# A differential-attention block: the gate multiplied on GpSimd as a group's values leave PSUM, and scores in chunks of 1024, 1024 and 256 keys

## The chip, the cores and the metric

The kernel runs on one core of a Trainium2 chip. The metric is the time on the device in microseconds, from the first to the last instruction and what lies around them. The core's engines work from queues of their own and meet at semaphores: TensorE (products and transposes into PSUM), VectorE, ScalarE and GpSimd (work on elements), and SyncE (SP), which here issues all DMA transfers.

## The reference

One block of a diffusion transformer with differential attention: 2048 latent tokens, 256 context tokens, a model width of 1024, 8 heads. Each head has two query and key maps of width 64 and values of width 128. Both softmaxes run over all 2304 keys.

```python
s = jnp.einsum('bqhzd,bkhzd->bhzqk', q, k)
p = jax.nn.softmax(s, axis=-1)
a = p[:, :, 0] - lam * p[:, :, 1]
o = jnp.einsum('bhqk,bkhe->bqhe', a, v)
...
of = of * lax.rsqrt(jnp.mean(of * of, axis=-1, keepdims=True) + SUBLN_EPS)
of = of * subln_gain * (1.0 - lambda_init)
y = (of.reshape(B, L, D) * jax.nn.silu(z)) @ w_out
...
return rms_norm(x + gt * y, final_gain)
```

Ahead of it stand a norm with modulation, one projection of width 4096 (queries, keys, values and the gate's z) and an axial rotation of queries and keys. All arithmetic has the accuracy of float32.

## The kernel before, in words

**Three stages.** `project` writes queries, keys, values and the gate (silu of z times `sgain`, transposed) to DRAM. `attend` computes the attention. `finish` multiplies by the output weights, adds x and applies the last norm.

**Attention.** A group is 256 queries of a head (`GQ`); there are 8 groups a head and 64 in all. A group consists of two halves `u` of 128 queries, and each half has two maps `z`; one half with one map is called a unit here. For a unit, `qk` (L671) computes the scores of 2304 keys in three chunks of 768. A chunk takes a score buffer of two PSUM banks; there are two such buffers (`S_BUFS`). Operands are split into a high and a low part, so each piece of keys gets two products (`f` = 0, 1), each of 384 columns. `keep` (L697) brings a chunk from PSUM to SBUF on VectorE and finds its least value on the way. `least`, `expo` (ScalarE, over all 2304 keys), `ratio`, then `weigh` and `join` on GpSimd (L726, L731) form the difference of both softmaxes.

The difference is then turned, 128 by 128, by TensorE (`turn`, L735; nine blocks a group), split into `hi` (ScalarE) and `lo` (VectorE, L751), and multiplied by the values in `pv` (L756) with products of 256 columns. After the ninth block `evac` (L768) copies the group's 128x256 result out of PSUM and stores it to `o_d`. `clamp`, `square`, `sq_high`, `sq_low` (GpSimd, L785), `sumsq` and `ssq_out` form the sum of squares, a row of which is stored for each group. At the end of a head `root` (GpSimd, nine small instructions from L823 to L831) turns the head's sums into factors, which `f_out` stores to `f_d`.

**Output.** For a block of 512 queries and each head, `Last.load` fetches the result, the gate and the factors into one of two sets of buffers (`o`, `gate`, `f`), 256 KB each. `mul1` (L968) multiplies by the factors on GpSimd, `mul2` (L972) by the gate on VectorE, `high` (L976) and `low` (L982) split the product into `gh` (ScalarE) and `gl` (VectorE). In `finish`, `mm` (L1020) multiplies with the output weights, with 512 columns. Heads 0 to 6 of the first block are prepared beside the attention of head 7; the others follow in `finish`.

**Order.** Each stage is written as steps with an engine, a cost in ns, a due time, dependencies and buffers to take and give. `Plan.order` (L128) plays these through and so fixes each engine's order once; `in_order` (L182) makes it binding. A letter in a plan stands for a pool of buffers: S the score buffers, T the blocks of `turn`, A and B the unit's scores, O the buffers of `Last`. Due times in `attend` count units of a third of a unit (`PER` = 12 a group). SP issues in the order in which the steps were written out, and waits at each transfer until its data and its buffer are ready.

Of the kernel before, what the change touches and what calls it, by code (L numbers as in the profile page):

```python
# [20 lines left out]
P = 128  # L21
# [4 lines left out]
KEYS = LAT + CTX  # L26
# [7 lines left out]
LN2 = math.log(2.0)  # L34
G = 2
GQ = G * P
CK = 768
NC = KEYS // CK
# [16 lines left out]
def build(tc, x, c, ctx, c_ctx, norm_gain, ada_w, ada_b, final_gain, w_in,  # L55
          lam_q, lam_k, subln_gain, w_out, cos_t, sin_t, out):
    nc = tc.nc
    with ExitStack() as top:
# [36 lines left out]
        last = Last(tc, gate_d, o_d, f_d, wo_d)  # L95
        ph = top.enter_context(ExitStack())
        with ExitStack() as inner:
            attend(tc, ph, inner, early, last, ident, ones, mhalf, sums, neglam, q_d, k_d, v_d, o_d, s_d, f_d)
# [94 lines left out]
def project(tc, ph, attend_early, ones, x, ctx, c, c_ctx, norm_gain, ada_w, ada_b, w_in, lam_q, lam_k, subln_gain,  # L193
# [296 lines left out]
    def z_gain(nm):  # L490
        nc.gpsimd.tensor_scalar(tiles["z", nm], tiles["z", nm], sgain[:, 0:1], 1.0, op0=ALU.mult, op1=ALU.mult)
# [151 lines left out]
def attend(tc, ph, inner, early, last, ident, ones, mhalf, sums, neglam, q_d, k_d, v_d, o_d, s_d, f_d):  # L643
# [27 lines left out]
    def qk(g, u, z, ck):  # L671
# [13 lines left out]
        for f in range(2):  # L685
            for b in range(2):
                k0 = ck * CK + b * (CK // 2)
                nc.tensor.matmul(ps[:, b, :CK // 2], group[g].q[:, z, f, u * P:(u + 1) * P],  # L688
                                 head[h].k[:, z, k0:k0 + CK // 2], start=(f == 0), stop=(f == 1))
                yield  # L690
# [6 lines left out]
    def keep(g, u, z, ck):  # L697
        un = unit[g, u]
        nc.vector.tensor_scalar(  # L699
            un.p[z][:, ck * CK:(ck + 1) * CK].rearrange("p (b k) -> p b k", b=2),  # L700
            un.s[z, ck][:, :, :CK // 2], -0.125, None, op0=ALU.mult, op1=ALU.min,
            accum_out=un.st[:, 3 * z + ck:3 * z + ck + 1])
# [32 lines left out]
    def turn(g, b):  # L735
        pt = ps_t.tile([P, 512], F32, tag="t", name=f"t{g}_{b}")
# [31 lines left out]
    def evac(g):  # L768
# [3 lines left out]
        nc.sync.dma_start(o_d[h][:, i * GQ:(i + 1) * GQ], group[g].o)  # L772

    def clamp(g):
        group[g].sq = op.tile([P, GQ], F32, tag="sq", name=f"sqo{g}")
        nc.gpsimd.tensor_scalar(group[g].sq, group[g].o, 2.0 ** 59, -(2.0 ** 59), op0=ALU.min, op1=ALU.max)

# [43 lines left out]
    def root(h):  # L821
# [4 lines left out]
        nc.gpsimd.tensor_scalar(hd.mk, hd.u, 2.0 ** 72, 1.0, op0=ALU.is_lt, op1=ALU.mult)  # L826
# [15 lines left out]
    plan = Plan(S=S_BUFS, T=T_BUFS, A=A_BUFS, B=2, HI=TP_BUFS, LO=TP_BUFS, O=2)  # L842
# [15 lines left out]
    for g in range(TOTAL):  # L858
        h = g // NG
        for u in range(G):  # L860
            for z in range(2):
                s0 = g * PER + (u * 2 + z) * NC
                for ck in range(NC):
                    take = ["S"] + (["AB"[z]] if ck == 0 else [])
                    step("qk", "PE", 700, s0 + ck, qk, (g, u, z, ck), take=take)
                    step("keep", "DVE", 865, s0 + ck + 0.5, keep, (g, u, z, ck), [("qk", g, u, z, ck)],
# [18 lines left out]
        step("clamp", "Pool", 1029, due + 6, clamp, (g,), [("evac", g)])  # L885
        step("square", "Activation", 307, due + 7, square, (g,), [("clamp", g)])
# [14 lines left out]
    for h in range(H - 1):  # L901
# [4 lines left out]
        step("gmul2", "DVE", 602, due + 5, last.mul2, (0, h), [("gmul1", 0, h)])  # L906
        step("ghigh", "Activation", 520, due + 6, last.high, (0, h), [("gmul2", 0, h)])
# [27 lines left out]
class Last:  # L935


    def __init__(self, tc, gate_d, o_d, f_d, wo_d):
# [3 lines left out]
        self.gate_d, self.o_d, self.f_d = gate_d, o_d, f_d  # L942
# [4 lines left out]
    def open(self):  # L947
        self.io = self.stack.enter_context(self.tc.tile_pool(name="gio", bufs=2, side="right"))
# [9 lines left out]
    def load(self, b, h):  # L958
        nc, sl = self.nc, slice(b * 512, (b + 1) * 512)
        o = self.io.tile([P, 512], F32, tag="o", name=f"o{b}_{h}")  # L960
        gate = self.io.tile([P, 512], F32, tag="gate", name=f"gate{b}_{h}")
        f = self.io.tile([P, 512], F32, tag="f", name=f"f{b}_{h}")
        nc.sync.dma_start(o, self.o_d[h][:, sl])
        nc.sync.dma_start(gate, self.gate_d[h][:, sl])
        nc.sync.dma_start(f, self.f_d[h][b * 4:b * 4 + 4].rearrange("a q -> (a q)").partition_broadcast(P))
        self.t[b, h] = SimpleNamespace(o=o, gate=gate, f=f)
# [20 lines left out]
def finish(tc, ph, last, x, final_gain, mhalf, gt_d, out):  # L987
# [10 lines left out]
    plan = Plan(O=2, Y=4, X=XB, V=YB, **{f"G{p}{h}": int(p) for p in range(2) for h in range(H)})  # L998
# [185 lines left out]
```

## Time and profile before

| | before |
|---|---|
| median of three runs | 2298.7 us (2296.99 to 2302.23) |
| the profiled execution's own time | 2306.51 us |
| its span, first to last instruction | 2304.3 us |
| mean granted clock of TensorE | 0.989 of full speed |
| TensorE, products | busy 2234.4 us, 97% of the span |
| VectorE | busy 1621.4 us, 70% |
| GpSimd | busy 1444.9 us, 63% |
| ScalarE | busy 1272.5 us, 55% |

The profile is of one execution. Its busy times of TensorE are modelled and overlap from product to product, so a rate is read from starts. A share over the whole span mixes three stages; a row of a single stretch says more. A wait that a row names is put down to the engine whose event came last.

### The profile page before, as it was taken

To read this page: it belongs to the slowest core of one execution; us is meant where nothing else is said; L and a number is where in the kernel's file an instruction comes from. 1 tells how busy PE (TensorE), PEld (TensorE's weight loads), DVE (VectorE), ACT (ScalarE), POOL (GpSimd) and SP (SyncE) were. 2 spreads that over 40 slices of the span, in tenths; PEclk is the share of its full clock that TensorE was granted. 3 is DMA by queue.
4 is the path that set the end of the run, shared out by engine and by line. 5 is a ranking of instruction groups with operands and counts; after the bars stand their busy time and mean duration, and the time that the engine had idled before them with its cause. 6 is when DMAs were issued, how large, how long until landed. Compare 5 with 4: busy or idle time off the path is not lost.

```text
span 2304.3 us, 37788 instructions
## 1 busy us (share of the span) xinstructions
PE 2234.4 (97%) x14353; PEld 2061.4 (89%) x14353; DVE 1621.4 (70%) x3486; ACT 1272.5 (55%) x1909; POOL 1444.9 (63%) x747
## 2 busy tenths in 40 slices
PE   6999999999999999999999999999999997899988
PEld 5987888898888879999999999999999997898777
DVE  6755434363323359998999989999899999884663
ACT  5612322132212148887888878888788885674221
POOL 2433233353322358888888888898888987784543
PEclk9999999999999999999999999999999999999999
DMA  9865644545443251231321412313214123215772
GB/s 310 287 221 189 224 145 170 165 132 176 136 137 110 92 178 35 51 102 35 77 77 35 117 36 51 102 36 76 77 35 116 37 57 112 70 44 186 229 231 83
DMA packets 201162, 275.45 MB, mean 120 GB/s; under 512 B 13469, under 2 KB 147221, under 8 KB 195861
## 3 DMA queue, kind: packets, MB, share of 16 engines
q1 hardware_dynamic: 200980, 273.04, 38.2%
q8 instruction: 113, 1.85, 0.3%
q14 instruction: 69, 0.56, 0.1%
HBM read 184.78 MB, written 88.22 MB: 118 GB/s over the span
## 4 chain that ended last, share of the span: by engine, by line
PE 69%; DVE 11%; ACT 6%; POOL 6%; DMA 4%; issue 4%; SPq 0%; POOLq 0%; ACTq 0%; DVEq 0%
PE s L688 15%; PE po L763 12%; PE t L740 7%; PE py L1033 5%; ACT p L717 4%; DVE p L699 4%; DVE lo L754 2%; POOL p L733 1%; DMA o<-od 1%; ACT hi L749 1%; PE m21vl L446 1%; PE m23vl L446 1%; PE m22vl L446 1%; PE m13vl L446 1%; PE m12vl L446 1%
## 5 line engine op out<-in xcount | busy, mean ns | idle before, releaser
L699 DVE TENSOR_SCALAR_CACHE_REDUCE p<-s 128x768 f32<-128x768 f32 x768 | 724.4, 951 | 64.2 <-PE s L688 56.1
L688 PE MATMUL s<-k,q 128*128 128x384 f32 x3072 | 700.1, 353 | 8.9 <-DVE p L699 7.3
L733 POOL TENSOR_TENSOR p<-p,p 128x2304 f32<-128x2304 f32 x128 | 663.4, 5183 | 10.3
L717 ACT ACTIVATE p<-p,st 128x2304 f32<-128x2304 f32 x256 | 569.7, 2225 | 165.9 <-DVE st L706 165.4
L688 PEld LDWEIGHTS s<-k,q 128*128 128x128 f32 x3072 | 508.2, 191 | 19.7 <-DVE p L699 17.7
L763 PE MATMUL po<-hi,v 128*128 128x256 f32 x2304 | 504.9, 286 | 0.0
L754 DVE TENSOR_TENSOR lo<-t,hi 128x512 fp32r<-128x512 f32 x576 | 389.7, 686 | 69.4 <-ACT hi L749 63.6
L729 POOL TENSOR_SCALAR p<-p,st 128x2304 f32<-128x2304 f32 x128 | 292.5, 2285 | 167.8 <-DVE st L721 110.1
L763 PEld LDWEIGHTS po<-hi,v 128*128 128x128 f32 x2304 | 394.8, 191 | 2.3 <-ACT hi L749 0.5
L749 ACT CAST hi<-t 128x512 fp32r<-128x512 f32 x576 | 323.3, 578 | 92.1 <-PE t L740 89.2
L740 PE MATMUL t<-ident,p 128*128 128x128 f32 x2304 | 347.5, 274 | 1.3 <-POOL p L733 1.3
L763 PE MATMUL po<-lo,v 128*128 128x256 f32 x1152 | 329.3, 286 | 19.2 <-DVE lo L754 19.2
L740 PEld LDWEIGHTS t<-ident,p 128*128 128x128 f32 x2304 | 276.7, 141 | 10.5 <-POOL p L733 1.6
L763 PEld LDWEIGHTS po<-lo,v 128*128 128x128 f32 x1152 | 220.1, 191 | 23.2 <-DVE lo L754 22.5
L1033 PE MATMUL py<-wo,gh 128*128 128x512 f32 (+1 forms) x528 | 164.2, 394 | 7.1 <-ACT gh L980 6.7
L1033 PEld LDWEIGHTS py<-wo,gh 128*128 128x128 f32 x528 | 98.9, 191 | 30.2 <-ACT gh L980 7.5
L1033 PE MATMUL py<-wo,gl 128*128 128x512 f32 (+1 forms) x264 | 103.9, 394 | 1.5 <-DVE gl L984 1.5
L980 ACT CAST gh<-o 128x512 fp32r<-128x512 f32 x32 | 19.8, 620 | 97.1 <-DVE o L974 94.2
L1046 POOL TENSOR_TENSOR fv<-fv,fx 128x512 f32<-128x512 f32 x30 | 42.3, 1423 | 42.0 <-DVE fv L1041 38.8
L699 DVE DVE_READ_ACCUMULATOR p<-s 128x1 f32 x768 | 63.5, 83 | 0.0
L974 DVE TENSOR_TENSOR o<-o,gate 128x512 f32<-128x512 f32 x32 | 41.0, 1283 | 31.3 <-POOL o L970 31.3
L1033 PEld LDWEIGHTS py<-wo,gl 128*128 128x128 f32 x264 | 50.3, 190 | 14.3 <-DVE gl L984 3.2
(593 smaller groups left out, 3893.5 us busy)
## 6 DMA issues: line engine op xcount, KB each, us to landing
q<-qd SPq DMA_DIRECT2D x256, 128.0 KB
k<-kd SPq DMA_DIRECT2D x32, 576.0 KB
v<-vd SPq DMA_DIRECT2D x16, 1152.0 KB
aw<-in_ada_w SPq DMA_DIRECT2D x12, 1024.0 KB
xl<-in_x SPq DMA_DIRECT2D x16, 512.0 KB
wod<-hlwo SPq DMA_DIRECT2D x16, 512.0 KB
od<-ot SPq DMA_DIRECT2D x64, 128.0 KB
o<-od SPq DMA_DIRECT2D x32, 256.0 KB
```

Source lines behind the costliest of these rows:

```text
L446: nc.tensor.matmul(tiles["m", nm][:, t * 256:(t + 1) * 256], tok[:, j, ts], ww[:, j], start=(i == 0), stop=(i == 3 * NCH - 1))
L688: nc.tensor.matmul(ps[:, b, :CK // 2], group[g].q[:, z, f, u * P:(u + 1) * P], head[h].k[:, z, k0:k0 + CK // 2], start=(f == 0), stop=(f = ...
L699: nc.vector.tensor_scalar(un.p[z][:, ck * CK:(ck + 1) * CK].rearrange("p (b k) -> p b k", b=2), un.s[z, ck][:, :, :CK // 2], -0.125, None, ...
L717: nc.scalar.activation(un.p[z], un.p[z], AF.Exp, bias=un.st[:, 6 + z:7 + z], scale=-1.0, accum_out=acc)
L729: nc.gpsimd.tensor_scalar(p[1], p[1], st[:, 9:10], st[:, 10:11], op0=ALU.mult, op1=ALU.mult)
L733: nc.gpsimd.tensor_tensor(p[0], p[0], p[1], op=ALU.add)
L740: nc.tensor.transpose(pt[:, (e * G + u) * P:(e * G + u + 1) * P], unit[g, u].p[0][:, kt * P:(kt + 1) * P], ident)
L749: nc.scalar.copy(t[1], t[0])
L754: nc.vector.tensor_tensor(t[2], t[0], f32(t[1]), op=ALU.subtract)
L763: nc.tensor.matmul(po, head[h].v[:, vi, kt], tt[:, e * GQ:(e + 1) * GQ], start=(kt == 0 and n == 0), stop=(kt == KT - 1 and n == 2))
L1033: nc.tensor.matmul(py[r, i], aa[:, ts], w[h][:, f, sl], start=(h == 0 and n == 0), stop=(h == H - 1 and n == 2))
L1046: eng.tensor_tensor(ys[r][:, sl], ys[r][:, sl], xs[r][:, sl], op=ALU.add)
```

## The change

There are two parts, which don't depend on each other.

First, a unit's scores are cut at 0, 1024, 2048 and 2304 keys. The two large chunks use products of 512 columns and fill both banks of a score buffer, the small one uses one product of 256 columns for each `f`. A unit's products fall from twelve to ten; chunks, evictions and buffers stay as many. The plan's costs and due times follow each chunk's share of the keys.

Second, the gate is multiplied onto a group's values right after the attention, by GpSimd, in a new step `gated` between `clamp` and `square`, and the store to `o_d` moves from `evac` behind that multiply. The gate of a group (128 KB) is loaded when its eighth block is turned, into one buffer. `mul2`, and the gate's 256 KB load in `Last.load`, go, and the `Last` buffers become three. So that the stored values stay in range, the gate is stored smaller by 2^35 (`F_SCALE`) and the factors are larger by as much. The buffers of `row` go from two to one.

```diff
-CK = 768
-NC = KEYS // CK
+CUTS = (0, 1024, 2048, KEYS)
+NC = len(CUTS) - 1
...
     def z_gain(nm):
-        nc.gpsimd.tensor_scalar(tiles["z", nm], tiles["z", nm], sgain[:, 0:1], 1.0, op0=ALU.mult, op1=ALU.mult)
+        nc.gpsimd.tensor_scalar(tiles["z", nm], tiles["z", nm], sgain[:, 0:1], 1.0 / F_SCALE, op0=ALU.mult, op1=ALU.mult)
...
         for f in range(2):
-            for b in range(2):
-                k0 = ck * CK + b * (CK // 2)
-                nc.tensor.matmul(ps[:, b, :CK // 2], group[g].q[:, z, f, u * P:(u + 1) * P],
-                                 head[h].k[:, z, k0:k0 + CK // 2], start=(f == 0), stop=(f == 1))
+            for b, k0 in enumerate(range(CUTS[ck], CUTS[ck + 1], 512)):
+                n = min(512, CUTS[ck + 1] - k0)
+                nc.tensor.matmul(ps[:, b, :n], group[g].q[:, z, f, u * P:(u + 1) * P],
+                                 head[h].k[:, z, k0:k0 + n], start=(f == 0), stop=(f == 1))
...
         nc.vector.tensor_scalar(
-            un.p[z][:, ck * CK:(ck + 1) * CK].rearrange("p (b k) -> p b k", b=2),
-            un.s[z, ck][:, :, :CK // 2], -0.125, None, op0=ALU.mult, op1=ALU.min,
+            un.p[z][:, CUTS[ck]:CUTS[ck + 1]],
+            un.s[z, ck].rearrange("p b k -> p (b k)")[:, :CUTS[ck + 1] - CUTS[ck]], -0.125, None,
+            op0=ALU.mult, op1=ALU.min,
...
     def turn(g, b):
+        if b == NB - 2:
+            h, i = divmod(g, NG)
+            group[g].gate = op.tile([P, GQ], F32, tag="gate", name=f"gate{g}", bufs=1)
+            nc.sync.dma_start(group[g].gate, gate_d[h][:, i * GQ:(i + 1) * GQ])
...
         nc.scalar.copy(group[g].o, po2[:, g % 2])
-        nc.sync.dma_start(o_d[h][:, i * GQ:(i + 1) * GQ], group[g].o)
...
+    def gated(g):
+        h, i = divmod(g, NG)
+        nc.gpsimd.tensor_tensor(group[g].o, group[g].o, group[g].gate, op=ALU.mult)
+        nc.sync.dma_start(o_d[h][:, i * GQ:(i + 1) * GQ], group[g].o)
...
-        row = op.tile([1, GQ], F32, tag="row", name=f"row{g}")
+        row = op.tile([1, GQ], F32, tag="row", name=f"row{g}", bufs=1)
...
-        nc.gpsimd.tensor_scalar(hd.mk, hd.u, 2.0 ** 72, 1.0, op0=ALU.is_lt, op1=ALU.mult)
+        nc.gpsimd.tensor_scalar(hd.mk, hd.u, 2.0 ** 72, F_SCALE, op0=ALU.is_lt, op1=ALU.mult)
...
-    plan = Plan(S=S_BUFS, T=T_BUFS, A=A_BUFS, B=2, HI=TP_BUFS, LO=TP_BUFS, O=2)
+    plan = Plan(S=S_BUFS, T=T_BUFS, A=A_BUFS, B=2, HI=TP_BUFS, LO=TP_BUFS, O=3)
...
-                    step("qk", "PE", 700, s0 + ck, qk, (g, u, z, ck), take=take)
-                    step("keep", "DVE", 865, s0 + ck + 0.5, keep, (g, u, z, ck), [("qk", g, u, z, ck)],
+                    share = (CUTS[ck + 1] - CUTS[ck]) / KEYS
+                    at = s0 + NC * CUTS[ck] / KEYS
+                    step("qk", "PE", 2070 * share, at, qk, (g, u, z, ck), take=take)
+                    step("keep", "DVE", 75 + 2380 * share, at + 1.5 * share, keep, (g, u, z, ck), [("qk", g, u, z, ck)],
...
         step("clamp", "Pool", 1029, due + 6, clamp, (g,), [("evac", g)])
+        step("gated", "Pool", 620, due + 7, gated, (g,), [("clamp", g)])
         step("square", "Activation", 307, due + 7, square, (g,), [("clamp", g)])
...
         step("gmul1", "Pool", 1250, due + 4, last.mul1, (0, h), [("gload", 0, h)])
-        step("gmul2", "DVE", 602, due + 5, last.mul2, (0, h), [("gmul1", 0, h)])
-        step("ghigh", "Activation", 520, due + 6, last.high, (0, h), [("gmul2", 0, h)])
+        step("ghigh", "Activation", 520, due + 6, last.high, (0, h), [("gmul1", 0, h)])
...
-        self.io = self.stack.enter_context(self.tc.tile_pool(name="gio", bufs=2, side="right"))
+        self.io = self.stack.enter_context(self.tc.tile_pool(name="gio", bufs=3, side="right"))
...
-        gate = self.io.tile([P, 512], F32, tag="gate", name=f"gate{b}_{h}")
...
-        nc.sync.dma_start(gate, self.gate_d[h][:, sl])
...
-    def mul2(self, b, h):
-        t = self.t[b, h]
-        self.nc.vector.tensor_tensor(t.o, t.o, t.gate, op=ALU.mult)
```

`finish` changes in the same way: its plan gets O=3, and its steps `gmul2` go.

## Rows read from the trace of the kernel before

**Rows 1.** The page's busy times: engine, busy us, share of the span, instructions.

```profile
PE 2234.4 (97%) x14353; PEld 2061.4 (89%) x14353; DVE 1621.4 (70%) x3486; ACT 1272.5 (55%) x1909; POOL 1444.9 (63%) x747
```

**Rows 2.** Busy us of each engine by stretch, then granted clock, DMA share, GB/s.

```profile
1300.00:1500.00 200.00, 199.43 (x1458) 195.63 (x1457) 180.42 (x451) 161.17 (x242) 171.67 (x71) 1.00 0.24 71
...
1900.00:2000.00 100.00, 83.11 (x534) 79.25 (x533) 92.76 (x177) 62.30 (x95) 74.67 (x37) 0.90 0.32 93
```

**Rows 3.** Line 771, two stretches: count, ns least/median/most, first and last start.

```profile
L771 ACT COPY ot<-po x52: 345/358/383, 894.9 to 1872.1; 128x256 f32<-128x256 f32 x52
...
L771 ACT COPY ot<-po x8: 347/358/377, 1891.4 to 2062.5; 128x256 f32<-128x256 f32 x8
```

**Rows 4.** Waits (total, times, longest): TensorE 900-1890, 1900-2060, from 2106; GpSimd from 2106.

```profile
PE po L763 <- DVE lo L754: 1.4, 3, 0.5
...
PE po L763 <- DVE lo L754: 17.9, 9, 3.6
...
PE py L1033 <- ACT gh L980: 6.7, 2, 5.5
...
POOL o L970 <- DMA o<-od: 26.7, 12, 4.6
```

**Rows 5.** Timeline of TensorE in the attention: start us, us, instruction, how many.

```profile
1307.07 0.28 PE L763 MATMUL po<-hi,v 128*128 128x256 f32 x1
...
1308.51 0.86 PE L688 MATMUL s<-k,q 128*128 128x384 f32 x4
1309.21 0.60 PE L740 MATMUL t<-ident,p 128*128 128x128 f32 x4
```

**Rows 6.** Timeline of TensorE in the projection; 21 starts left out between.

```profile
339.81 0.39 PE L434 MATMUL m12ql<-lol,wh12q 128*128 128x512 f32 x1
...
344.80 0.39 PE L434 MATMUL m12ql<-hil,wl12q 128*128 128x512 f32 x1
```

**Rows 7.** Timeline of TensorE in the output; 18 products from start to start.

```profile
2169.89 0.63 PE L1033 MATMUL py<-wo,gh 128*128 128x512 f32 x2
...
2174.09 0.63 PE L1033 MATMUL py<-wo,gh 128*128 128x512 f32 x2
```

**Rows 8.** Groups by line, 900 to 1900: count, busy us, mean ns, idle before.

```profile
L699 DVE TENSOR_SCALAR_CACHE_REDUCE p<-s 128x768 f32<-128x768 f32 x627 | 591.2, 951 | 30.6 <-PE s L688 26.0 <-PE pss L792 2.6
...
L754 DVE TENSOR_TENSOR lo<-t,hi 128x512 fp32r<-128x512 f32 x470 | 318.5, 686 | 54.5 <-ACT hi L749 49.4
...
L787 POOL TENSOR_TENSOR sh<-sqo,sh 128x256 fp32r<-128x256 f32 x52 | 38.8, 747 | 0.0
```

**Rows 9.** Timeline of GpSimd around the end of a head, idle time before in brackets.

```profile
1318.68 0.40 POOL L776 TENSOR_SCALAR sqo<-ot 128x256 f32<-128x256 f32 x1
1320.32 2.28 POOL L729 TENSOR_SCALAR p<-p,st 128x2304 f32<-128x2304 f32 x1 [1.23 <-DVE st L721]
...
1344.34 2.28 POOL L729 TENSOR_SCALAR p<-p,st 128x2304 f32<-128x2304 f32 x1
```

**Rows 10.** Groups by line on VectorE, 1900 to 2060.

```profile
L974 DVE TENSOR_TENSOR o<-o,gate 128x512 f32<-128x512 f32 x8 | 18.0, 2249 | 3.0 <-POOL o L970 3.0
L984 DVE TENSOR_TENSOR gl<-o,gh 128x512 fp32r<-128x512 f32 x7 | 17.8, 2541 | 0.0
```

**Rows 11.** Timelines of VectorE, GpSimd and TensorE in head 7.

```profile
1923.61 4.79 DVE L984 TENSOR_TENSOR gl<-o,gh 128x512 fp32r<-128x512 f32 x1
...
1922.75 5.10 POOL L733 TENSOR_TENSOR p<-p,p 128x2304 f32<-128x2304 f32 x1
...
1929.05 0.58 PE L763 MATMUL po<-lo,v 128*128 128x256 f32 x1 [3.58 <-DVE lo L754]
```

**Rows 12.** By stretch, after TensorE's longest wait in the output.

```profile
2208.00:2215.00 7.00, 5.38 (x12) 3.83 (x13) 5.34 (x7) 2.58 (x6) 2.55 (x2) 0.54 0.75 261
```

**Rows 13.** Timeline of TensorE: three chunks of scores, 1300 to 1304.

```profile
1300.75 1.65 PE L688 MATMUL s<-k,q 128*128 128x384 f32 x8
...
1303.30 0.95 PE L688 MATMUL s<-k,q 128*128 128x384 f32 x4
```

More of the change, by code (lines that the diff above doesn't have):

```diff
@@ L34 @@
 LN2 = math.log(2.0)
+F_SCALE = 2.0 ** 35
 G = 2
 GQ = G * P
-CK = 768
-NC = KEYS // CK
+CUTS = (0, 1024, 2048, KEYS)
+NC = len(CUTS) - 1
 LAG = 10
@@ L93, in build @@
                     cos_t, sin_t, ident, mhalf, sgain, neglam, gt_d, q_d, k_d, v_d, gate_d, w_out, wo_d, sums)
-        last = Last(tc, gate_d, o_d, f_d, wo_d)
+        last = Last(tc, o_d, f_d, wo_d)
         ph = top.enter_context(ExitStack())
         with ExitStack() as inner:
-            attend(tc, ph, inner, early, last, ident, ones, mhalf, sums, neglam, q_d, k_d, v_d, o_d, s_d, f_d)
+            attend(tc, ph, inner, early, last, ident, ones, mhalf, sums, neglam, q_d, k_d, v_d, gate_d, o_d, s_d, f_d)
         with ExitStack() as inner:
@@ L640, in load_q, with attend @@
     return qt
-def attend(tc, ph, inner, early, last, ident, ones, mhalf, sums, neglam, q_d, k_d, v_d, o_d, s_d, f_d):
+def attend(tc, ph, inner, early, last, ident, ones, mhalf, sums, neglam, q_d, k_d, v_d, gate_d, o_d, s_d, f_d):
     nc = tc.nc
@@ L935, with __init__ @@
 class Last:
-    def __init__(self, tc, gate_d, o_d, f_d, wo_d):
+    def __init__(self, tc, o_d, f_d, wo_d):
         self.tc, self.nc = tc, tc.nc
@@ L941, in __init__ @@
         self.w = {}
-        self.gate_d, self.o_d, self.f_d = gate_d, o_d, f_d
+        self.o_d, self.f_d = o_d, f_d
         self.stack = ExitStack()
@@ L960, in load @@
         o = self.io.tile([P, 512], F32, tag="o", name=f"o{b}_{h}")
-        gate = self.io.tile([P, 512], F32, tag="gate", name=f"gate{b}_{h}")
         f = self.io.tile([P, 512], F32, tag="f", name=f"f{b}_{h}")
         nc.sync.dma_start(o, self.o_d[h][:, sl])
-        nc.sync.dma_start(gate, self.gate_d[h][:, sl])
         nc.sync.dma_start(f, self.f_d[h][b * 4:b * 4 + 4].rearrange("a q -> (a q)").partition_broadcast(P))
-        self.t[b, h] = SimpleNamespace(o=o, gate=gate, f=f)
+        self.t[b, h] = SimpleNamespace(o=o, f=f)
     def mul1(self, b, h):
@@ L997, in finish @@
     XB, YB = 3, 3
-    plan = Plan(O=2, Y=4, X=XB, V=YB, **{f"G{p}{h}": int(p) for p in range(2) for h in range(H)})
+    plan = Plan(O=3, Y=4, X=XB, V=YB, **{f"G{p}{h}": int(p) for p in range(2) for h in range(H)})
     done = {}
@@ L1088, in heads_steps @@
         step("gmul1", "Pool", 1250, due - 6, last.mul1, (b, h), [("gload", b, h)])
-        step("gmul2", "DVE", 602, due - 5, last.mul2, (b, h), [("gmul1", b, h)])
         take = [f"G{b % 2}{h}"] if b else []
-        step("ghigh", "Activation", 520, due - 4, last.high, (b, h), [("gmul2", b, h)], take=take)
+        step("ghigh", "Activation", 520, due - 4, last.high, (b, h), [("gmul1", b, h)], take=take)
         step("glow", "DVE", 602, due - 4, last.low, (b, h), [("ghigh", b, h)], give=["O"])
```

## The prediction

> **What bounds the kernel now.** I read the page first: TensorE is busy for 97% of the span [rows 1], so a gain must come from products that take less time or from stretches in which TensorE stands. A modelled busy time can hide either, so the table by stretches comes next [rows 2]. In the middle of the attention TensorE is busy for 199.4 of 200 us, with VectorE at 180.4 and GpSimd at 171.7: TensorE sets the pace, and VectorE follows 10% behind. From 1900 to 2000 it is busy for only 83.1 of 100 us at a granted clock of 0.90, while VectorE shows 92.8. That is head 7, beside which the loads and products of `Last` for heads 0 to 6 already run. So there are three stages with different limits: seven heads paced by TensorE, head 7, and the output products.
>
> The pace itself is not read from durations (they overlap) but from starts. A pass over the 64 groups: 52 evacuations from 894.9 to 1872.1 us give 977.2 / 51 = 19.16 us for a group; the seven intervals from 1891.4 to 2062.5 take 171.1 us, which at 19.16 would be 134.1 [rows 3]. Head 7 therefore loses 37 us. TensorE's waits name by whom [rows 4]: nearly nobody in the steady part (1.4 us in 990), VectorE's `lo` in head 7 (17.9 us), ScalarE's `gh` in the output (6.7 us, one wait of 5.5).
>
> **Scores in chunks of 1024, 1024 and 256.** A unit (128 queries, one of the two maps) has twelve products of 384 columns now; it gets eight of 512 and two of 256. The number of chunks (3), of evictions and of streamed columns stays. The price of a product is its distance to the next start. Four of 384 columns take 1309.21 - 1308.51 = 0.70 us, 175 ns each; twelve of 256 columns in `pv` take 1308.51 - 1307.07 = 1.44 us, 120 ns each [rows 5]. Products of 512 stand in two places: in the projection 22 of them take 344.80 - 339.81 = 4.99 us, 227 ns each [rows 6]; in the output 18 take 2174.09 - 2169.89 = 4.20 us, 233 ns each [rows 7]. No trace of this kernel shows 512 columns streaming from the keys, so these two are the bounds. A unit now: 12 x 175 = 2.10 us. After, at 227: 8 x 227 + 2 x 120 = 2.056 us, 44 ns less; at 233: 2.104 us, 4 ns more. I take 227, because the attention's own 175 and 120 fit it: they are 15 and 13 ns above their columns at 2.4 GHz, and 227 is 14 above. Over 4 units and 56 groups (head 7 is counted below) that is 224 x 44 ns = 10 us off; with 233 it is 1 us on.
>
> A rule of the Trainium skill speaks against this part. "TensorE: Matmul & The Clock Gate", section "Wait — 56ns, not 53.3ns?", gives back-to-back products a fixed cost of about 2.5 ns beside the columns at 2.4 GHz. By it a unit would fall from 1.950 to 1.945 us, an estimate of 1 us in the whole kernel in place of 10. The rows above show 13 to 15 ns instead; the measurement decides.
>
> The eviction `keep` costs VectorE 951 ns for 768 columns, and `lo` 686 for 512 [rows 8]: 1.035 ns a column, leaving 156 fixed. So 1024 columns are 1216 and 256 are 421, and a unit's sum stays at 2.85 us. Cost nothing, with one reservation in the first rival.
>
> **The gate moves to GpSimd, group by group.** New for each group: a load of 128 KB issued on SP at the last turn but one, a multiply of 128x256 on GpSimd between `clamp` and `sqlow`, and the store to `o_d` behind that multiply rather than behind `evac`. Its price is that of `sqlow`, the same form: 747 ns [rows 8], 64 times. What hides it: after `clamp` (0.40 us at 1318.68) GpSimd stands idle for 1.23 us until `weigh` may start at 1320.32 [rows 9]. The 0.75 us fits, and `weigh` and `join`, queued behind, start as before. That cover is missing once per head: after the chain of `root`, `weigh` starts at 1344.34 without any idle time [rows 9]. There 0.75 us is pushed onto `weigh`, `join` and the turns that wait for them, at most 7 x 0.75 = 5 us; since TensorE shows no wait for `join` in the steady part [rows 4], I take 1 us, with 0 and 5 as ends.
>
> The gate tile has one buffer, so its load waits for the previous group's multiply, about a period earlier: no wait. Behind it on SP stand the next `q` load and the row of squares, each due within the period. It has about 2/9 of a period (19.16 x 2/9 = 4.3 us) and the evacuation and `clamp` on top before the multiply needs it; the longest wait of GpSimd for a load in the crowded output is 4.6 us [rows 4]. If it lands late, GpSimd waits with `weigh` behind it, and the 1.23 us absorb the first of that. I take 0. The changed constants (`F_SCALE`) ride in instructions that exist: 0. ScalarE's `row` with one buffer waits for a store a period old: 0.
>
> **What goes in head 7.** Removed: `gmul2` on VectorE. From 1900 to 2060 eight of them take 18.0 us, 2249 ns each, and seven subtractions `gl` 17.8 us [rows 10]. An estimate of either unhindered is 0.69, from `lo` of the same width [rows 8], so 12 to 13 us of each group are waiting inside the instruction. Why can be seen at 1923: `gl` runs from 1923.61 for 4.79 us while GpSimd's `join` runs from 1922.75 for 5.10, and ends when `join` does; TensorE's next product then starts 3.58 us late [rows 11]. `lo` and `keep`, with an operand in PSUM, aren't stretched beside the same joins. Such a hold can't be caught up by an engine with 10% to spare, and the granted clock falls behind it: 37 us lost against 35.8 us in these two groups. Removing `gmul2` takes out half of the cause: 37 x 18.0 / 35.8 = 18.6, I take 18 us off. Ends: 5.5 (eight at 0.69, with the held time passing to whoever comes next) and 30 (the remaining `gl` also fall into better moments). What is late next there is still `gl`. `gmul1` now feeds `gh` directly, so a late GpSimd stops ScalarE and the `hi` copies behind it, rather than VectorE.
>
> **What goes in the output.** There the ring of two `o` buffers is the limit: load, `gmul1`, `gmul2`, `gh`, `gl`, load again. GpSimd waits 26.7 us for the load, and TensorE 5.5 us at once for `gh` [rows 4], after which the clock stands at 0.54 for 7 us [rows 12], 7 x 0.46 = 3.2 us lost. With three buffers, one step fewer in the ring and no 256 KB gate load beside it, this wait should vanish: 5.5 + 3.2, I take 9 off; ends 0 and 10 (all 6.7 us of `gh`). TensorE is then the bound up to the last block, whose end is unchanged.
>
> **Sum.** -10 - 18 - 9 + 1 = -36 us. The profiled execution took 2306.5 us, 2.2 more than its span, so it would become 2270.5. The median of the three timed runs, 2298.7, lies 7.8 below it, so I forecast 2263.
>
> **Rivals.** (1) *The two score buffers* become the limit, and the kernel slower. A chunk's buffer is free after its products, one `lo` that may stand ahead, and its `keep`: with 768 columns the trace shows products at 1300.75 and the next use of that buffer at 1303.30, 2.55 us [rows 13]. With 1024 that is 0.21 more for products (4 x 52 ns) and 0.265 for `keep`: 3.02 us. Between the second chunk of a unit and the first of the next, which takes over its buffer, lie 1280 of 2304 keys: 2.66 us of the 4.79 if TensorE's other work is spread evenly. TensorE would wait 0.36 us, 92 us over 256 units. It decides from 36 / 256 = 0.14 us a unit, two fifths of that; with three fifths the time is 2263 + 55 = 2318. Against it: in two units (9.58 us) each buffer serves three chunks, two of 1024 and one of 256, and 3.02 + 3.02 + 1.6 = 7.6 is as much as three times 2.55 now, and the present order already puts two chunks back to back (eight products at 1300.75 [rows 13]), so the other work needn't be even. For it: only two buffers, and VectorE at 90%. (2) *512 columns run at the output's pace* of 233: no 10 us, +1: 2274. (3) *Head 7 keeps its loss*, as `gl` takes the hold that `gmul2` had: 5.5 instead of 18: 2275. (4) *Head 7 mends further*, 30 us: 2251. That the output stays bound by its loads (0 for 9) gives 2272 and lies within the forecast's own range, 2252 to 2274.
>
> **How the numbers follow.** Forecast 0.50, rival 1 0.18, rival 2 0.10, rival 3 0.12, rival 4 0.10. A measurement tells some 0.2% from no change, 4.6 us. All but rival 1 end below 2294: 0.82 faster. Rival 1 is a matter of degree; I give 0.04 to a wait near the deciding point (same) and 0.14 to slower. The range runs from 2246, below rival 4, to 2298, with the case where rival 1 eats the gain; 0.14 above and 0.03 below are left out.
>
> **What would show it.** Right: starts of 512-column score products 227 ns apart and groups at 18.98 us; GpSimd's gate multiply at 0.75 us in the idle time ahead of `weigh`; evacuations of head 7 about 2.6 us a group closer; no wait of some us for `gh` in the output. Wrong: score products waiting for `keep` in the steady part (rival 1), 233 ns (2), `gl` beyond 2.5 us each with seven intervals still near 165 us (3). A gate load that lands after `clamp`, with `weigh` late in every group, would break the part on GpSimd, which no rival prices.

## The result, and the profile after

The changed kernel takes 2267.7 us (median of four runs, 2266.1 to 2273.1) beside 2299.2 for the kernel before: 31.5 less. The measured ratio is 0.9847 with a 95% interval of 0.9825 to 0.9869, which is 35 us; the quotient of the two medians, 0.9863, lies inside the interval. The forecast was 2263 within 2246 to 2298. The profiled execution took 2266.1 us with a span of 2264.4, which is 39.9 less than the span of before. That is more than the kernels differ by, since the profiled execution of before, with 2306.5 us, was 7.3 slower than its median. So differences of a few us between the two profiles can belong to the executions.

Where the 39.9 us lie is read from the evacuations of the groups' results, as in [rows 3]. Three stretches of line 777 of the changed kernel (line 771 before), columns as there: the first 53 intervals, the seven of head 7, and head 7 with the last three behind it.

```profile
L777 ACT COPY ot<-po x54: 370/372/373, 873.3 to 1888.8; 128x256 f32<-128x256 f32 x54
...
L777 ACT COPY ot<-po x8: 344/372/372, 1888.8 to 2034.2; 128x256 f32<-128x256 f32 x8
...
L777 ACT COPY ot<-po x11: 344/372/373, 1888.8 to 2078.2; 128x256 f32<-128x256 f32 x11
```

The same from the kernel before: its first 53 intervals, and its last twelve evacuations.

```profile
L771 ACT COPY ot<-po x54: 345/358/387, 875.7 to 1891.4; 128x256 f32<-128x256 f32 x54
...
L771 ACT COPY ot<-po x12: 347/360/377, 1872.1 to 2106.6; 128x256 f32<-128x256 f32 x12
```

| stretch | before | after | difference | forecast |
|---|---|---|---|---|
| start to the first evacuation | 875.7 | 873.3 | -2.4 | 0 |
| 53 intervals, heads 0 to 6 | 1015.7 | 1015.5 | -0.2 | -10 + 1 |
| seven intervals, head 7 | 171.1 | 145.4 | -25.7 | -18 |
| the last three | 44.1 | 44.0 | -0.1 | 0 |
| last evacuation to the end of the span | 197.7 | 186.2 | -11.5 | -9 |

The first row is untouched work: over all kernels here the first score product starts anywhere between 822 and 833 us, so differences of some us there belong to the execution and not to the edit. The steady part brought nothing. Head 7 brought most, more than forecast.

Groups by line on VectorE and GpSimd of the changed kernel, 900 to 1880 us, the lines that answer to [rows 8]:

```profile
L700 DVE TENSOR_SCALAR_CACHE_REDUCE p<-s 128x1024 f32<-128x1024 f32 x410 | 499.4, 1218 | 51.8 <-PE s L689 43.1
L700 DVE TENSOR_SCALAR_CACHE_REDUCE p<-s 128x256 f32<-128x256 f32 x204 | 84.6, 415 | 1.0
...
L785 POOL TENSOR_TENSOR ot<-ot,gate 128x256 f32<-128x256 f32 x51 | 37.8, 741 | 3.3
```

An eviction of 1024 columns takes 1218 ns (1216 worked out), one of 256 takes 415 (421), the gate's multiply 741 (747).

The pace of the scores, in TensorE's timeline (start, duration, instruction, how many), answers to [rows 5]:

```profile
1197.26 1.09 PE L689 MATMUL s<-k,q 128*128 128x512 f32 x4
1198.19 0.28 PE L769 MATMUL po<-hi,v 128*128 128x256 f32 x1
```

Four products of 512 columns take 0.93 us: 232.5 ns each, the pace of the output [rows 7] and not of the projection [rows 6].

GpSimd's timeline at a group's end, beside [rows 9] (idle time before in brackets):

```profile
1181.28 0.40 POOL L781 TENSOR_SCALAR sqo<-ot 128x256 f32<-128x256 f32 x1
1181.77 0.74 POOL L785 TENSOR_TENSOR ot<-ot,gate 128x256 f32<-128x256 f32 x1
1183.18 2.28 POOL L731 TENSOR_SCALAR p<-p,st 128x2304 f32<-128x2304 f32 x1 [0.67 <-PE s L689]
```

The multiply stands behind `clamp` in time that was idle, and 0.67 us of the idle time remain ahead of `weigh`. Nothing waits for the gate's load.

Head 7: what is left of `Last` on VectorE from 1885 to 2060, beside [rows 10]:

```profile
L990 DVE TENSOR_TENSOR gl<-o,gh 128x512 fp32r<-128x512 f32 x7 | 13.1, 1870 | 0.0
```

TensorE's waits (total, times, longest) from 1890 to 2060 and, as the last line, from 2078 to the end, beside [rows 4]:

```profile
PE po L769 <- DVE lo L760: 3.2, 2, 2.9
PE pss L802 <- POOL sh L797: 2.8, 1, 2.8
PE s L689 <- DVE p L700: 2.2, 3, 1.0
...
PE pss L802 <- POOL sh L797: 0.8, 1, 0.8
```

Busy times of two stretches of the output, columns as in [rows 2, 12]:

```profile
2110.00:2160.00 50.00, 50.00 (x216) 40.24 (x215) 36.48 (x46) 14.94 (x35) 37.17 (x30) 1.00 0.67 212
2160.00:2210.00 50.00, 50.00 (x216) 40.25 (x215) 28.13 (x40) 12.69 (x29) 27.70 (x23) 1.00 0.58 192
```

`gmul2` is gone, and most of TensorE's waits for `lo` with it: they fall from 17.9 to 3.2 us. In the output TensorE no longer waits for `gh` at all, and the granted clock stays at 1.00 in both stretches.

Head 7 again, from 1890 to 2050 us, columns as in [rows 2], before and after:

```profile
1890.00:2050.00 160.00, 137.53 (x901) 131.57 (x900) 143.93 (x295) 103.50 (x158) 121.81 (x57) 0.91 0.32 90
...
1890.00:2050.00 160.00, 151.93 (x1028) 136.24 (x1027) 146.68 (x346) 127.14 (x185) 148.90 (x75) 0.99 0.30 88
```

In these 160 us TensorE stood for 22.5 us before and for 8.1 after, 14.4 less. The granted clock rose from 0.91 to 0.99, and 0.08 of 160 us is another 13 us. So about half of head 7's gain is what the lower clock no longer costs. GpSimd is busy for 93% of the stretch after the change, 76% before.

### The profile page after: what moved, and what is told of

Its sections match the earlier page's. It is cut to its first block, busy times and chain, and to the rows that moved or that the text cites. A ratio compares the mean times of both kernels' runs of the same rounds, so it can differ in the third digit from the quotient of the medians.

```text
span 2264.4 us, 36796 instructions
## 1 busy us (share of the span) xinstructions
PE 2214.5 (98%) x13841; PEld 1956.7 (86%) x13841; DVE 1588.8 (70%) x3454; ACT 1300.0 (57%) x1909; POOL 1493.7 (66%) x811
## 4 chain that ended last, share of the span: by engine, by line
PE 82%; POOL 6%; DVE 5%; DMA 3%; issue 3%; ACT 1%; SPq 0%; POOLq 0%; ACTq 0%; DVEq 0%
PE s L689 20%; PE po L769 16%; PE t L746 9%; PE py L1039 8%; POOL p L735 2%; DVE p L700 2%; POOL p L731 1%; PE m23vl L447 1%; PE m22vl L447 1%; PE m21vl L447 1%; PE m13vl L447 1%; PE m12vl L447 1%; PE m11vl L447 1%; PE m20vl L447 1%; PE m13zl L435 1%
## 5 line engine op out<-in xcount | busy, mean ns | idle before, releaser
L700 DVE TENSOR_SCALAR_CACHE_REDUCE p<-s 128x1024 f32<-128x1024 f32 (+1 forms) x768 | 727.8, 950 | 86.7 <-PE s L689 75.9
L689 PE MATMUL s<-k,q 128*128 128x512 f32 (+1 forms) x2560 | 690.3, 387 | 11.6 <-DVE p L700 11.5
L769 PE MATMUL po<-hi,v 128*128 128x256 f32 x2304 | 510.3, 288 | 0.0
L689 PEld LDWEIGHTS s<-k,q 128*128 128x128 f32 x2560 | 423.4, 189 | 66.1 <-DVE p L700 18.9
L755 ACT CAST hi<-t 128x512 fp32r<-128x512 f32 x576 | 332.9, 581 | 149.2 <-PE t L746 137.5
L746 PEld LDWEIGHTS t<-ident,p 128*128 128x128 f32 x2304 | 271.5, 140 | 20.5 <-POOL p L735 0.8
L769 PEld LDWEIGHTS po<-lo,v 128*128 128x128 f32 x1152 | 218.8, 190 | 17.8 <-DVE lo L760 4.5
L1056 ACT ACTIVATE fx<-fv 128x512 f32<-128x512 f32 (+1 forms) x33 | 20.4, 620 | 90.1 <-POOL fv L1052 83.2
L990 DVE TENSOR_TENSOR gl<-o,gh 128x512 fp32r<-128x512 f32 x32 | 40.6, 1289 | 16.7 <-ACT gh L986 16.4
```

The lines of the kernel that those rows point to most:

```text
L689: nc.tensor.matmul(ps[:, b, :n], group[g].q[:, z, f, u * P:(u + 1) * P], head[h].k[:, z, k0:k0 + n], start=(f == 0), stop=(f == 1))
L700: nc.vector.tensor_scalar(un.p[z][:, CUTS[ck]:CUTS[ck + 1]], un.s[z, ck].rearrange("p b k -> p (b k)")[:, :CUTS[ck + 1] - CUTS[ck]], -0.12 ...
L746: nc.tensor.transpose(pt[:, (e * G + u) * P:(e * G + u + 1) * P], unit[g, u].p[0][:, kt * P:(kt + 1) * P], ident)
L755: nc.scalar.copy(t[1], t[0])
L769: nc.tensor.matmul(po, head[h].v[:, vi, kt], tt[:, e * GQ:(e + 1) * GQ], start=(kt == 0 and n == 0), stop=(kt == KT - 1 and n == 2))
```

## The experiments

Each kernel was timed beside the kernel before on the same chip. That kernel's median there was 2299 to 2305 us, so ratios are compared, and stages by their profile, one execution of each kernel. The seven intervals of head 7 would be 134.1 us at the steady rate (1015.5 / 53 x 7); what they take beyond it is called the loss.

**The two parts alone.** First the chunks, in the kernel before, then the gate, as the changed kernel with the old chunks.

```diff
-CK = 768
-NC = KEYS // CK
+CUTS = (0, 1024, 2048, KEYS)
+NC = len(CUTS) - 1
```

> The kernel before with the score chunks of 1024, 1024 and 256 keys alone; multiply, loads and buffers of the gate as before. Theory of the prediction (512 columns take 227 ns, as in the projection): groups of head 1 to 6 at 18.98 us, the time 10 us below before, about 2289. Rival (512 columns take 233 ns, as in the output and as the changed kernel's trace shows in the scores): a unit's products stay at 2.10 us, the time lies within 3 us of before, 2296 to 2302, and head 7 keeps its loss of 37 us (seven intervals 165 to 177 us).

```diff
-CUTS = (0, 1024, 2048, KEYS)
-NC = len(CUTS) - 1
+CK = 768
+NC = KEYS // CK
```

> The changed kernel with chunks of 768 keys and products of 384 columns again, so the gate's part alone. Theory of the prediction: -18 in head 7, -9 in the output, +1 for the ends of heads, about 2272, 5 us above the changed kernel. Rival (the chunks bring nothing, the gate's part brings all): 2264 to 2270, not above the changed kernel by more than 2 us; seven intervals of head 7 near 146 us, TensorE without a wait of some us for gh in the output.

The chunks alone gave 2290.2 us, a ratio of 0.9941 (0.9925 to 0.9957); the gate alone 2273.4 us, 0.9864 (0.9846 to 0.9882). Both times are near those of the theory of the prediction, but the kernel before took 2305.1 us beside them: by the ratios the gains are 13.6 and 31 us, where the theory has 10 and 26. They add up to more than the 35 of both parts together. The stages tell another story than the theory. The evacuations of the chunks alone, then of the gate alone, in the first 53 intervals and in head 7:

```profile
L772 ACT COPY ot<-po x54: 360/372/374, 881.3 to 1896.7; 128x256 f32<-128x256 f32 x54
...
L772 ACT COPY ot<-po x8: 351/372/373, 1896.7 to 2051.9; 128x256 f32<-128x256 f32 x8
```

```profile
L776 ACT COPY ot<-po x54: 344/367/373, 877.3 to 1897.3; 128x256 f32<-128x256 f32 x54
...
L776 ACT COPY ot<-po x8: 347/368/375, 1897.3 to 2041.9; 128x256 f32<-128x256 f32 x8
```

With the chunks alone the steady part is 1015.4 us, 0.3 less than before: no gain. What they gained lies in head 7, 155.2 us instead of 171.1 (the rival had 165 or more), where the same multiplications and subtractions of `Last` run, but at other moments: the fifteen instructions took 35.8 us before [rows 10], and here 28.8:

```profile
L977 DVE TENSOR_TENSOR o<-o,gate 128x512 f32<-128x512 f32 x8 | 19.2, 2394 | 0.1
L987 DVE TENSOR_TENSOR gl<-o,gh 128x512 fp32r<-128x512 f32 x7 | 9.6, 1373 | 0.0
```

With the gate alone head 7 has its whole gain (144.6), so the two parts overlap there and don't add up. The steady part is 4.3 us longer than before. So beside the gate the chunks are worth 4.5 us in the steady part, though alone they are worth nothing. Each edit makes the planner write a new order for all engines. Why the order with both is as good as the old one, and the one with the gate alone isn't, was not settled.

**Without gmul2.** The multiplication by the gate is left out; its loads and the two sets of buffers stay.

```diff
     def mul2(self, b, h):
-        t = self.t[b, h]
-        self.nc.vector.tensor_tensor(t.o, t.o, t.gate, op=ALU.mult)
+        return None
```

> The kernel before without the instruction gmul2 (the multiplication by the gate is left out, its loads remain, two sets of buffers). If VectorE held behind GpSimd's join makes head 7's loss, the seven intervals fall from 171 to 145-153 us, and with a few us in the output the time is 2268 to 2278. If the loads beside head 7, or the amount of work on VectorE at its unhindered 0.69 us, make the loss, they stay at 163 us or more and the time at 2288 or more.

2280.2 us, 0.9900 (0.9881 to 0.9918). Head 7's seven intervals, and the last evacuation at 2090.2:

```profile
L771 ACT COPY ot<-po x8: 349/358/375, 1887.9 to 2046.1; 128x256 f32<-128x256 f32 x8
...
L771 ACT COPY ot<-po x11: 349/359/375, 1887.9 to 2090.2; 128x256 f32<-128x256 f32 x11
```

The time of `gl` in head 7, in the groups by line on VectorE:

```profile
L984 DVE TENSOR_TENSOR gl<-o,gh 128x512 fp32r<-128x512 f32 x7 | 20.7, 2956 | 0.0
```

Head 7 falls by 12.9 us to 158.2, in the middle between both theories (153 and 163); the time is nearer to that of the hold. `gl` took 20.7 us here, more than before (17.8): all seven were held, five before. What `gmul2` and `gl` take together beyond 0.69 us each fell from 25.4 to 15.9 us, so a good part of the hold stayed. GpSimd also stood for 8.2 us for loads of `o` from 1890 to 2060 (2.5 before), a part of the loss that may belong to the loads. The output falls from 197.7 to 187.1 us, with the gate's loads still there and with two sets of buffers. So leaving out that one step is worth 10.6 of the 11.5 us of the output.

**Two sets of buffers instead of three.**

```diff
-    plan = Plan(S=S_BUFS, T=T_BUFS, A=A_BUFS, B=2, HI=TP_BUFS, LO=TP_BUFS, O=3)
+    plan = Plan(S=S_BUFS, T=T_BUFS, A=A_BUFS, B=2, HI=TP_BUFS, LO=TP_BUFS, O=2)
...
-        self.io = self.stack.enter_context(self.tc.tile_pool(name="gio", bufs=3, side="right"))
+        self.io = self.stack.enter_context(self.tc.tile_pool(name="gio", bufs=2, side="right"))
```

> The changed kernel with two sets of buffers (o, f) instead of three, in the pool and in both plans. If the ring of two sets limits the output, TensorE waits some us for gh there again and the clock falls: 4 to 9 us above the changed kernel, 2271 to 2277. If one step fewer in the ring is enough, the time stays within 2 us of the changed kernel, 2266 to 2270.

2266.5 us, 0.9838 (0.9819 to 0.9857). GpSimd waits 20.9 us for loads of `o` in the output again (3.8 with three sets), and TensorE's only wait there stays the 0.8 us for a sum of squares. The waits of GpSimd, then of TensorE, from 2076 to the end (total, times, longest):

```profile
POOL o L980 <- DMA o<-od: 20.9, 6, 8.3
...
PE pss L802 <- POOL sh L797: 0.8, 1, 0.8
```

So the third set is worth nothing that the measurement tells: the ring without `gmul2` is short enough. In head 7 the seven `gl` of this kernel took the same times as those of the changed kernel within 0.03 us each, and the seven intervals 144.4 us instead of 145.4. About 1 us is thus what one order gives from one execution to another.

**What is left of head 7's loss.** After the change 145.4 - 134.1 = 11.3 us are left. Six kernels looked for their cause, four of them here. In the first, joins of head 7 are two instructions; in the second, `gl` beside head 7 runs on GpSimd.

```diff
-        nc.gpsimd.tensor_tensor(p[0], p[0], p[1], op=ALU.add)
+        if g < (H - 1) * NG:
+            nc.gpsimd.tensor_tensor(p[0], p[0], p[1], op=ALU.add)
+        else:
+            for i in range(2):
+                sl = slice(i * KEYS // 2, (i + 1) * KEYS // 2)
+                nc.gpsimd.tensor_tensor(p[0][:, sl], p[0][:, sl], p[1][:, sl], op=ALU.add)
```

> The changed kernel; in head 7 each join is issued as two instructions of 1152 columns, so that nothing can be held behind one for more than about 2.6 us. Theory (gl is held behind join, and head 7 loses some 1.4 us for each us held): gl falls from 13.1 us in seven to 7-10, none above 2.8 us (now 4.07 and 2.91), the seven intervals from 145.4 to 138-142 us, the time 3 to 7 us below the changed kernel. Rival (what is left of head 7's loss, 12 us, comes from GpSimd being full, 94% busy): the intervals stay at 145 us or grow, as two instructions cost more than one.

```diff
-        step("glow", "DVE", 602, due + 7, last.low, (0, h), [("ghigh", 0, h)], give=["O"])
+        step("glow", "Pool", 1250, due + 7, last.low, (0, h), [("ghigh", 0, h)], give=["O"])
...
-        self.nc.vector.tensor_tensor(t.lo, t.o, f32(t.hi), op=ALU.subtract)
+        eng = self.nc.gpsimd if (b == 0 and h < H - 1) else self.nc.vector
+        eng.tensor_tensor(t.lo, t.o, f32(t.hi), op=ALU.subtract)
```

> The changed kernel; the seven subtractions gl beside head 7 run on GpSimd (some 1.29 us each) instead of VectorE. Theory (the hold of VectorE is the loss): no VectorE instruction with two SBUF operands is left there, TensorE's waits for lo vanish, the seven intervals fall to 134-139 us, the time 6 to 11 us below the changed kernel. Rival (GpSimd, 94% busy, is the next limit): 9 us more on GpSimd push weigh and join back, the turns wait, and the intervals stay above 143 us.

In both runs the theory failed and the rival, GpSimd as the next limit, has its number. With halves: 2265.7 us, 0.9834 (0.9809 to 0.9859), `gl` 10.9 us in seven, the seven intervals 144.8. With `gl` on GpSimd: 2269.1 us, 0.9856 (0.9831 to 0.9881), intervals 143.5. In both the hold is shorter or gone and the loss is nearly as large. TensorE's waits in head 7, 1890 to 2060, show what stood in its place, first with halves, then with `gl` on GpSimd (the longest of each):

```profile
PE pss L807 <- POOL sh L802: 3.9, 2, 3.3
PE s L689 <- DVE p L700: 3.2, 5, 1.2
```

```profile
PE pss L802 <- POOL sh L797: 4.1, 2, 3.0
PE po L769 <- DVE lo L760: 1.3, 2, 0.7
```

TensorE stands at the product `pss` of a group's sum of squares, which it must do in the written order, while GpSimd still has `sqlow` ahead of it, behind other work. That is how a full GpSimd reaches TensorE: from 1890 to 2050 it is busy for 152.6 of 160 us with halves and for 153.3 with `gl` on it. In the changed kernel's seven intervals it is busy for 136.5 of 145.4 us, which is more than 134.1. So with this work on GpSimd the seven intervals can't fall to 134.1, and at least 2.4 of the 11.3 us are GpSimd's. Whether all of them are was not tested: no run took work off it.

Then the due times of `Last`'s steps beside head 7 were shifted, nothing else.

```diff
-        due = ((H - 1) * NG + h) * PER
+        due = ((H - 1) * NG + h) * PER + 3
```

> The changed kernel; the steps of Last beside head 7 are due 3 chunks later, nothing else. Theory (where a gl falls against a join is chance, and the loss follows the time held): gl sums to anything from 8 to 20 us, and the seven intervals are 133.4 us plus 1.2 to 1.6 times what gl takes beyond 0.69 us each, so anything from 138 to 156. Rival (the loss belongs to the loads and the number of steps): 145 within 1.5 us, whatever gl takes.

```diff
-        due = ((H - 1) * NG + h) * PER
+        due = ((H - 1) * NG + h) * PER + 6
```

> The changed kernel; the steps of Last beside head 7 are due 6 chunks later, nothing else. Theory, as for the shift by 3: seven intervals at 133.4 us plus 1.2 to 1.6 times the time that gl is held, another sum than with 0 or 3. Rival: 145 within 1.5 us.

With 3 the time was 2267.0 us (ratio 0.9842, 0.9810 to 0.9875), `gl` 14.7 us, the intervals 147.4: `gl` was held for 14.7 - 7 x 0.69 = 9.9 us, and the loss of 147.4 - 134.1 = 13.3 is 1.35 times that, as the theory has it. With 6 it was 2277.1 (0.9886, 0.9842 to 0.9930) and the intervals 153.8, with `gl` at only 12.2 us: 7.4 us held and a loss of 19.7. The rival fell (it said 145), and so did the rule of the theory. TensorE's waits in head 7 of the kernel shifted by 6:

```profile
PE pss L802 <- POOL sh L797: 9.4, 2, 6.0
```

Its timeline at the longest of them, GpSimd and then TensorE:

```profile
2002.77 1.26 POOL L980 TENSOR_TENSOR o<-o,f 128x512 f32<-128x512 f32 x1 [6.37 <-DMA o<-od]
2003.99 0.72 POOL L797 TENSOR_TENSOR sh<-sqo,sh 128x256 fp32r<-128x256 f32 x1
...
2004.76 0.37 PE L802 MATMUL pss<-sh,ones 128*2 128x256 f32 x1 [6.03 <-POOL sh L797]
```

GpSimd waits 6.37 us for a load of `Last`, `sqlow` stands behind that instruction, and TensorE stands at `pss` for 6.03 us. A load that comes late reaches TensorE by two queues.

**The sum of squares later.** In TensorE's order of head 7 the product `pss` was moved back by about a third of a group, alone and together with the halves.

```diff
-        step("sumsq", "PE", 220, due + 9, sumsq, (g,), [("sqlow", g)], take=["T"])
-        step("ssq", "Activation", 380, due + 9, ssq_out, (g,), [("sumsq", g)], give=["T"])
+        later = 8 if (H - 1) * NG - 1 < g < TOTAL - 1 else 0
+        step("sumsq", "PE", 220, due + 9 + later, sumsq, (g,), [("sqlow", g)], take=["T"])
+        step("ssq", "Activation", 380, due + 9 + later, ssq_out, (g,), [("sumsq", g)], give=["T"])
```

> The changed kernel; in head 7 (all but the last group) TensorE's sum of squares is due 8 chunks later in the plan, so its product stands about a third of a group later in TensorE's order. Theory (what head 7 still loses is partly TensorE standing at that product, 2.8 us in the changed kernel and 6.0 us with the due times shifted by 6, while GpSimd still has sqlow ahead behind other work): no wait of TensorE for sh is left in head 7, the seven intervals fall from 145.4 to 139-142 us, the time 3 to 6 us below the changed kernel. Rival (the loss is VectorE held behind join, and the order of the sum changes nothing or moves the holds): 144 us or more.

> The later sum of squares and the joins of head 7 in two instructions together. Theory (two causes side by side: a hold of up to 5 us, and the wait for the sum): with neither, the seven intervals fall to 135-140 us (133.4 would be no loss), the time 5 to 10 us below the changed kernel. Rival (GpSimd full, 94% busy, is what remains): 143 us or more, as with the halves alone (144.8).

Alone: 2267.5 us, 0.9848 (0.9826 to 0.9870). The seven intervals of head 7:

```profile
L777 ACT COPY ot<-po x8: 352/372/372, 1887.1 to 2028.9; 128x256 f32<-128x256 f32 x8
```

TensorE's longest waits in that stretch:

```profile
PE s L689 <- DVE p L700: 2.7, 5, 1.0
PE po L769 <- ACT hi L755: 1.9, 2, 1.1
```

No wait for `sh` is left, and the seven intervals are 141.8 us, 3.6 below the changed kernel, the number that the theory has. But they don't lie where the wait was. TensorE's two longest waits in head 7 of the changed kernel:

```profile
1991.02 0.28 PE L802 MATMUL pss<-sh,ones 128*2 128x256 f32 x1 [2.80 <-POOL sh L797]
2016.13 0.39 PE L769 MATMUL po<-lo,v 128*128 128x256 f32 x1 [2.89 <-DVE lo L760]
```

The first falls into the sixth interval, which took 21.8 us there and takes 21.9 now, with new waits for `hi` and `lo` in it. The second falls into the seventh, which goes from 23.8 to 19.8: its `gl` had taken 4.07 us and now takes 2.25. So the gain is that of a shorter hold, as the rival has it (an order that moves the holds), though the rival's 144 us are not; the wait at `pss` was worth nothing that shows here. The total doesn't show it: 0.9848 stands beside 0.9847, with intervals of 0.4% around both. With the halves as well the intervals are 143.3 us and the time 2263.4, 0.9832 (0.9811 to 0.9853); the two cures don't add up, and the rival of that run (GpSimd as the limit, 143 us or more) has its number. No version tried is faster than the changed kernel by more than the measurement tells.

## Why the prediction was right, and where it wasn't

The sum was right within 5 us (2263 for 2267.7), though two of its three large terms were mis-sized and made up for each other. That they did is luck.

**Scores, -10: the term failed.** The step that failed is the choice between two bounds, 227 ns from the projection and 233 from the output. It rested on 227 being 14 ns above its columns, as 175 and 120 are 15 and 13 above theirs. The products came at 232.5, the pace of the rejected bound, and a unit costs 8 x 232.5 + 2 x 120 = 2.10 us, what it cost before. Rival 2 had this right. Both bounds were rows of the same 512 columns, and the argument by widths was weaker than it looked: it used two widths to choose the pace of a third. What makes the projection's products 6 ns shorter was not found. The rule of the Trainium skill ("TensorE: Matmul & The Clock Gate", "Wait — 56ns, not 53.3ns?") gave an estimate of 1 us for this part and so came nearer to the result than my 10, but not for its reason: 232.5 ns are 19 above 512 columns at 2.4 GHz, where it has about 2.5.

The price of 175 ns for 384 columns left something out besides. Of a run of score products that follows four transposes, the second starts 261 ns after the first, 86 more than the rest; with 512 columns it is 320, 87 more. Both kernels pay this where scores follow transposes.

The sign that I had named, groups at 18.98 us, did come, and says less than it seems. The 19.16 it was worked out from is a mean over normal groups and heads' ends. Of the 53 intervals, the 47 normal ones took 19.08 us on average before and 19.02 after; the six at heads' ends took 19.82 before and 20.27 after. So 2.9 us were won and 2.7 given back. The evacuations around the second head's end, first before, then after:

```profile
1181.71 0.37 ACT L771 COPY ot<-po 128x256 f32<-128x256 f32 x1
1201.57 0.34 ACT L771 COPY ot<-po 128x256 f32<-128x256 f32 x1
```

```profile
1159.83 0.37 ACT L777 COPY ot<-po 128x256 f32<-128x256 f32 x1
1178.81 0.37 ACT L777 COPY ot<-po 128x256 f32<-128x256 f32 x1
1199.10 0.37 ACT L777 COPY ot<-po 128x256 f32<-128x256 f32 x1 [0.66 <-PE po L769]
1218.11 0.37 ACT L777 COPY ot<-po 128x256 f32<-128x256 f32 x1
```

19.86 before; 18.98, then 20.29, then 19.01 after. The chunks alone show the same, so it isn't the gate's multiply behind `root` for which I had put 1 us. Two kinds of waits of TensorE are named from 900 to 1885 after the change, six times each, once a head:

```profile
PE s L689 <- DVE p L700: 1.3, 6, 0.2
PE pf L845 <- POOL u L841: 1.2, 6, 0.3
```

The first of them is rival 1, the score buffers. Its 0.2 us is what the modelled busy time leaves; the starts show 0.45:

```profile
1188.37 0.60 PE L746 MATMUL t<-ident,p 128*128 128x128 f32 x4
1189.18 1.19 PE L689 MATMUL s<-k,q 128*128 128x512 f32 x4 [0.21 <-DVE p L700]
```

Elsewhere the scores start 0.36 us after the first of four transposes (three steps of 109 ns and 28 ns more), here 0.81. So rival 1 came true at 0.45 us a head in place of 0.36 a unit. A head's end lost as much, 20.27 for 19.82; the wait at `pf` stands beside it, and what makes up for that was not traced. The argument against it held within a head: per buffer the chain is no longer than before.

**GpSimd's gate multiply, 0 to 1: right.** 741 ns, in idle time, no wait for its load; the heads' ends are as long with the chunks alone. With the old chunks the steady part grew by 4.3 us all the same (the gate alone), a cost within the 5 us that I gave as an end, though by the order and not at the heads' ends alone.

**Head 7, -18: right in kind, too small.** It was 25.7, within the ends of 5.5 and 30. The mechanism is borne out where the hold is long: held time, what `gmul2` and `gl` take beyond 0.69 us each, was 25.4 us before (loss 37.0), 18.4 with the chunks alone (21.1), 15.9 without `gmul2` (24.1) and 8.3 after (11.3). The loss is more than the hold because the clock falls with it: TensorE's standing and the clock's share, summed over the seven intervals, give 36.1 of the 37.0 us, 18.5 of 21.1, 23.2 of 24.1 and 9.8 of 11.3. The prediction named the clock, but gave it no price. Below some 8 us the hold isn't the main cause any more: with `gl` on GpSimd VectorE holds nothing, and 143.5 - 134.1 = 9.4 us were still lost. What was mis-sized is that the share of `gmul2` was taken as 18.0 of 35.8 with `gl` unchanged. Leaving out `gmul2` alone gave 12.9, as `gl` grew to 20.7; in the changed kernel `gl` fell to 13.1. Where a `gl` falls against a `join` depends on an order that every edit rewrites, and the shifted due times moved head 7 by 2.0 and 8.4 us. So about half of the 25.7 us, the 12.8 beyond what leaving out `gmul2` gave, came with the rest of the change: the new order, and the gate's loads that no longer run beside head 7. Which of the two was not tested; that the order's part is chance is an argument from those shifts, not shown. What I had named as late next, `gl`, was only part of it: GpSimd at 93%, and TensorE's waits at `pss` behind it (2.8 us after, 9.4 with the due times shifted by 6), were not in the prediction.

**Output, -9: right.** It was 11.5, beyond my end of 10, which held TensorE's waits for `gh` (6.7 us) and the clock behind them (3.2). It left out the waits for `gl`, which stood beside those for `gh` [rows 4]:

```profile
PE py L1033 <- DVE gl L984: 1.5, 3, 0.8
```

They are gone as well, and 6.7 + 3.2 + 1.5 is 11.4. The attribution was partly wrong: of the three causes named (third set, one step fewer, no gate load), the missing step alone gave 10.6, and the third set nothing.

## What to carry to other kernels

Price a new form of instruction by the row of the stage in which it will run, and where only other stages show that form, give the bounds equal weight before a pattern over widths decides. An engine that is held inside an instruction by another engine's long one shows it as a duration far above its shortest; sum that excess over the stage before asking how busy the engine is. Then add up TensorE's standing and what the granted clock takes: the second can be as large as the first. When work moves from one engine to another in a crowded stage, sum the other engine's work there too; that sum is a floor. And where an order is planned anew with each edit, part of any gain in a crowded stage is luck: shift a due time by a little and see how much moves.

## What the runs showed of the hardware that was not expected

The pace of a product of 512 columns isn't one number in one kernel at one granted clock: 227 ns in the projection, 232.5 in the scores, 233 in the output. In the scores it alternates by head, about 231.9 and 232.9 in turn. In the output it did not follow how busy the other engines were: both stretches above have 216 products in 50 us, the one with 37.2 us of GpSimd and 36.5 of VectorE, the other with 27.7 and 28.1. Its cause stays open.

An instruction of VectorE with two operands in SBUF that started while GpSimd's `join` ran was held until the `join` had ended, up to 5.62 us for some 0.69 us of work, and then took 0.55 us more: in [rows 11] `join` ends at 1927.85 and `gl` at 1928.40. It isn't `join` alone. `gl` here stands behind `weigh`, which ends at 1909.51, and ends at 1910.04; the second line is the longest hold, of `gmul2` beside a `join` from 1937.34 to 1942.43:

```profile
1908.51 1.53 DVE L984 TENSOR_TENSOR gl<-o,gh 128x512 fp32r<-128x512 f32 x1
...
1937.35 5.62 DVE L974 TENSOR_TENSOR o<-o,gate 128x512 f32<-128x512 f32 x1
```

Every such instruction above 0.8 us in head 7, in all the kernels, ends 0.54 to 0.56 us behind the GpSimd instruction that ran beside its start. Instructions with an operand in PSUM never were held: `lo` took at most 695 ns beside the same joins. The Trainium skill has this as a rule ("SBUF — State Buffer", "Who interferes with whom"): a VectorE instruction with two SBUF inputs contends with a GpSimd instruction that reads SBUF, and the shared ports are an exclusive lock. The trace agrees: 4.79 us for `gl` beside a `join` of 5.10 [rows 11]. What the runs add is the price one level up: in the kernels with 8 to 25 us held, head 7 lost 1.1 to 1.5 us for each of them, the clock included. With less held other causes stand beside it: 7.4 us held went with 19.7 lost when the due times were shifted by 6.
